# Norm factors moved into the exponentials, four weight blocks side by side at the start, and a fused last product

## The chip, the cores and the metric

The kernel runs on one core of a Trainium2 chip. The metric is the device time of one execution in microseconds (us). TensorE (PE) does the matmuls, VectorE (DVE) and ScalarE (ACT) the elementwise work, GpSimd (POOL) a little of it, and SyncE (SP) and ACT issue the transfers (DMA) between memory and the core. Each engine runs its own instructions in order and waits for others by semaphores.

## The reference

One decoder layer for 256 tokens of width 1024, all in float32:

```
hn = rmsnorm(h, mix_norm_g);  proj = hn @ w_in
a, b, q, k_c, v_c, k_s, v_s, k_w, v_w, gates = split(proj)
y_conv = silu(layernorm(depthwise_conv31(a * sigmoid(b))))
y_nsa  = gated sum of compressed, selected and window attention (8 heads of 64)
h = h + concat(y_conv, y_nsa) @ w_out
h = h + memory_attention(rmsnorm(h, mem_q_norm_g), rmsnorm(mem, mem_kv_norm_g))   # 4 heads of 256
h = h + peer(rmsnorm(h, peer_norm_g))   # 8 heads, top 16 of 128 x 128 keys, 16384 experts
out = rmsnorm(h, final_norm_g)
```

An RMS norm multiplies each token by its gain per channel and by one factor, rsqrt(mean(x*x) + eps). The factor of a token is the same for all channels, so it can be applied after the matmul, and for attention scores it can be applied to the score instead of to the query.

## The kernel before

Activations lie transposed: 128 channels on the partitions, 256 tokens along the row, eight such chunks (`KC` = 8) for a width of 1024. `hx` is x times the gain. A projection block gives 128 output channels and sums over the eight chunks. `proj1` does a block as eight float32 matmuls (16 passes of PE in the trace). `proj`, by `mm3` (L152 to L154), splits weight and activation into a high part (`hi`, made by ACT) and a rest (`lo`, made by DVE at L142) and does 24 matmuls. Weight blocks of 512 KB come in through `wload`, in four `raw` buffers; `hi` and `lo` have six buffers each.

The order on PE is the order in which the program is written. The order on DVE, ACT and SP is decided by a scheduler that knows estimated durations; each engine then keeps to it strictly.

At the start PE runs 14 warm-up matmuls, then blocks in pairs, `pb` and `pa` (the gate and the value of the convolution branch). For a norm, the class `Rstd` sums squares (`sa_`), `sums()` adds them over the partitions on PE (`ss_`), computes the factor on DVE in a chain of 13 small steps and makes two diagonal matrices (`dg_`). `rows()` spreads the factor over a row by matmuls with these (`sr_`), which ACT copies (`rs_`). The suffix is x for the input, m for the memory, h for the two later norms, c for the convolution's layer norm.

`conv_in` (L302 to L307) makes the convolution's input from `pb`, `pa` and the row of factors. The convolution itself is 124 instructions on DVE, called taps here (`yc`, L296 and L298), which the scheduler spreads over the next 100 us as filler between the splits `lo`, the scaling of memory keys (`mkt`, L440) and the maxima of the attention scores (`amx`, L559). When all taps are done, `lsum` (L607 to L610) adds the four channel groups and PE takes the mean over channels (`pmu`, L616).

Further on come the memory queries (`pmq`, eight chunks; `mq_out` scales and splits them), the expert layer's queries (`ppq`, sixteen chunks), the key scores and top-k, and then the experts' matmuls (`pu`, `pw`, `Y`), which fill the time from some 312 us to the end. At the end, each half of 128 tokens is normed from the two PSUM banks `Y` by L1049 to L1064 (`fz` the result, `fm` the factor, `fj` the squares).

Of the kernel before, what the change touches and what calls it, by code (L numbers as in the profile page):

```python
# [51 lines left out]
def constants():  # L52
# [44 lines left out]
def build(tc, A, out, dbg=None):
# [99 lines left out]
    class Rstd:  # L197
# [16 lines left out]
        def sums(self):  # L214
# [9 lines left out]
            rsqrt(y, m, t, sh)  # L224
            self.diag = mwk.tile([P, 2, P], F32, name=f"dg_{self.tag}", tag="rs_d", bufs=1)
# [85 lines left out]
    pend = []  # L311
    for i in range(4):
        pb = psum(T, f"pb{i}")
        wb = wload(A["w_in_t"][2 * i]) if i else w0
        proj1(pb, wb, hx)
        if i == 1:
            r0.sums()
        wa = wload(A["w_in_t"][2 * i + 1])
        if i == 0:
            nc.sync.dma_start(con1, A["con"][:, 0:NCON1])  # L320
        pa = psum(T, f"pa{i}")
        proj1(pa, wa, hx, range(4))
        if i == 1:
            r0.rows()
            conv_in(*pend)
# [845 lines left out]
```

## Time and profile before

| | |
|---|---|
| median of three runs | 1082.49 us (1081.4 to 1082.73) |
| the profiled execution | 1082.72 us |
| its span | 1080.9 us |
| PE, DVE, ACT, POOL busy | 1061.2, 871.8, 580.0, 102.3 us |

The span runs from the first to the last event of the trace, and 1.8 us of the time lie outside it. PE is busy in 98% of it. [...] DVE is busy in 81% over the whole: in eight or nine tenths of most slices up to some 700 us, and in six tenths after that. In the timeline, the number in brackets is how long the engine was idle before the instruction, and what ended that. The difference between two starts (the pitch) can be less than an instruction's length, since neighbours overlap.

### The profile page before, as it was taken

The numbers are of one execution on the slowest core, as the hardware profiler recorded it, in microseconds if no ns is written. First come the engines' busy times: TensorE is split into PE (matmuls) and PEld (weight loads), VectorE is DVE, ScalarE is ACT, GpSimd is POOL, SyncE is SP. The second block draws the span as 40 slices with busy tenths as digits, with TensorE's granted clock in tenths as the row PEclk, the third lists the DMA queues.
The fourth block names the chain that finished last, engine by engine and source line by source line (L and its number), as shares of the span: only waits on it lengthen the run. The fifth ranks groups of instructions, "written<-read, shape, count | busy, mean of one in ns | idle before, by whom it ended". The sixth has DMA issues, their size and how long they took to land.

```text
span 1080.9 us, 20534 instructions
## 1 busy us (share of the span) xinstructions
PE 1061.2 (98%) x7346; PEld 976.3 (90%) x7346; DVE 871.8 (81%) x2226; ACT 580.0 (54%) x1334; POOL 102.3 (9%) x82
## 2 busy tenths in 40 slices
PE   8999999999999999999999999999999999999997
PEld 7889878999999999999999999998888888888885
DVE  4998888978889998889999999986666666666665
ACT  4224676566455555665555555455555555555554
POOL 0000000000039992000000000001000000000000
PEclk9999999999999999999999999999999999999999
DMA  7744333525435555444554444466555555555552
GB/s 245 247 127 151 98 99 117 196 98 174 159 116 178 178 193 167 160 162 157 162 164 163 163 150 160 156 203 201 194 190 193 194 192 192 195 194 193 195 195 78
DMA packets 51685, 182.45 MB, mean 169 GB/s; under 512 B 5760, under 2 KB 6528, under 8 KB 51456
## 3 DMA queue, kind: packets, MB, share of 16 engines
q1 hardware_dynamic: 51296, 180.62, 50.8%
q8 instruction: 58, 0.95, 0.4%
q10 hardware_dynamic: 288, 0.52, 0.1%
q14 instruction: 43, 0.35, 0.1%
HBM read 179.81 MB, written 1.05 MB: 167 GB/s over the span
## 4 chain that ended last, share of the span: by engine, by line
PE 85%; DVE 13%; ACT 1%; DMA 1%; issue 0%; SPq 0%; DVEq 0%; ACTq 0%
PE Y L1071 32%; PE pu L152 9%; PE pu L154 8%; PE pu L153 8%; PE pq L163 2%; PE pw L1017 1%; PE ppq L152 1%; PE ppq L153 1%; PE ppq L154 1%; PE pb L163 1%; PE pw L1018 1%; PE pa L163 1%; DVE ohx L948 1%; PE pmk L152 1%; DVE lo L142 1%; DVE ohx L946 1%
## 5 line engine op out<-in xcount | busy, mean ns | idle before, releaser
L141 ACT ACTIVATE hi<-raw 128x512 fp32r<-128x512 f32 x624 | 376.7, 626 | 176.7 <-PE pu L153 66.9
L142 DVE TENSOR_TENSOR lo<-raw,hi 128x512 fp32r<-128x512 f32 x556 | 369.1, 687 | 26.8 <-ACT hi L141 21.0
L152 PE MATMUL pu<-hn_h,hi 128*128 128x256 f32 x1024 | 296.3, 289 | 0.0
L154 PE MATMUL pu<-hn_h,lo 128*128 128x256 f32 x1024 | 290.7, 284 | 1.9 <-DVE lo L142 1.9
L153 PE MATMUL pu<-hn_l,hi 128*128 128x256 f32 x1024 | 290.7, 284 | 0.0
L154 PEld LDWEIGHTS pu<-hn_h,lo 128*128 128x128 f32 x1024 | 197.3, 193 | 2.1 <-DVE lo L142 2.1
L153 PEld LDWEIGHTS pu<-hn_l,hi 128*128 128x128 f32 x1024 | 197.4, 193 | 0.0
L152 PEld LDWEIGHTS pu<-hn_h,hi 128*128 128x128 f32 x1024 | 197.2, 193 | 0.0
L1071 PE MATMUL Y<-hi,al 128*128 128x512 f32 x512 | 158.3, 389 | 0.0
L1071 PE MATMUL Y<-lo,ah 128*128 128x512 f32 x512 | 158.3, 389 | 0.0
L1071 PE MATMUL Y<-hi,ah 128*128 128x512 f32 x512 | 158.2, 389 | 0.0
L1071 PEld LDWEIGHTS Y<-hi,al 128*128 128x128 f32 x512 | 96.1, 188 | 20.0
L1071 PEld LDWEIGHTS Y<-lo,ah 128*128 128x128 f32 x512 | 96.1, 188 | 19.9
L1071 PEld LDWEIGHTS Y<-hi,ah 128*128 128x128 f32 x512 | 96.1, 188 | 19.8
L167 DVE TENSOR_TENSOR al<-slB,ah 128x256 fp32r<-128x256 f32 x88 | 37.4, 425 | 86.1 <-PE Y L1071 86.1
L166 ACT ACTIVATE ah<-slB 128x256 fp32r<-128x256 f32 x88 | 36.8, 418 | 110.7 <-PE Y L1071 110.7
L142 POOL TENSOR_TENSOR lo<-raw,hi 128x512 fp32r<-128x512 f32 x68 | 94.8, 1421 | 11.8 <-ACT hi L141 9.2
L1023 ACT ACTIVATE slB<-pw 128x348 f32<-128x348 f32 (+31 forms) x64 | 32.5, 507 | 70.2 <-DVE slB L1022 57.0
L298 DVE SCALAR_TENSOR_TENSOR yc<-u,par,yc 128x256 f32<-128x256 f32 x120 | 54.8, 474 | 0.1
L167 DVE TENSOR_TENSOR al<-slA,ah 128x256 fp32r<-128x256 f32 x40 | 17.1, 428 | 37.3 <-PE Y L1071 37.3
L166 ACT ACTIVATE ah<-slA 128x256 fp32r<-128x256 f32 x40 | 16.7, 418 | 49.3 <-PE Y L1071 48.0
L152 PE MATMUL ppq<-gx_h,hi 128*128 128x256 f32 x128 | 37.4, 292 | 0.0
(372 smaller groups left out, 1745.7 us busy)
## 6 DMA issues: line engine op xcount, KB each, us to landing
raw<-u SPq DMA_DIRECT2D x128, 512.0 KB, 3.4
raw<-v SPq DMA_DIRECT2D x128, 512.0 KB, 3.3
raw<-peer_w_q SPq DMA_DIRECT2D x16, 512.0 KB, 3.3
raw<-w_in_t SPq DMA_DIRECT2D x15, 512.0 KB, 3.8
raw<-w_mem_k SPq DMA_DIRECT2D x8, 512.0 KB, 4.5
raw<-w_mem_v SPq DMA_DIRECT2D x8, 512.0 KB, 3.3
raw<-w_out SPq DMA_DIRECT2D x8, 512.0 KB, 3.4
raw<-w_mem_q SPq DMA_DIRECT2D x8, 512.0 KB, 3.5
```

The lines of the kernel that those rows point to most:

```text
L141: S.activation(hi, r, AF.Copy)
L142: (engs or (V, V))[q].tensor_sub(lo, r, hi.bitcast(F32))
L152: PE.matmul(ps, w[0], xh, start=start, stop=False)
L153: PE.matmul(ps, w[0], xl, start=False, stop=False)
L154: PE.matmul(ps, w[1], xh, start=False, stop=stop)
L163: PE.matmul(ps, w[0][:, k * P:(k + 1) * P], x[:, k], start=k == 0, stop=k == KC - 1)
L166: S.activation(dst[0], src, AF.Copy)
L167: V.tensor_sub(dst[1], src, dst[0].bitcast(F32))
L298: V.scalar_tensor_tensor(yc[:, i], u[:, i, j:j + T], w, yc[:, i], op0=ALU.mult, op1=ALU.add)
L946: V.tensor_tensor(o4, o4, tif[:, side].unsqueeze(2).to_broadcast([P, 16, 16, 8]), op=ALU.mult)
L1023: S.activation(slB[:, done - J:, n0:n0 + 4].rearrange("p i n -> p n i"), pw[:, :, done:], AF.Copy, scale=1.0 / GSC)
L1071: PE.matmul(Y[nh][c], lhs[:, sl], wc[c][t], start=False, stop=i == KEYS - 1 and lhs is a[1], skip_group_check=True)
```

## The change

There are five parts. (1) At the start the first four blocks are computed side by side: in each of the eight chunks, one matmul for each of four accumulators (`acc`). Their weights come in 16 transfers of 128 KB on SP, into tiles `wf` that use buffers of `hi` and `lo`; x comes in four transfers that ACT issues. The sums of squares follow behind the four blocks and the row of factors behind the fifth. The rope constants (`posf`, `ang`, `kk`, `St`, `Ct`), which stood at the very start, come after the input blocks; the second part of the constants (`con2`, with the causal mask among others) is loaded behind the last four blocks. (2) The NSA queries `qraw` stay without the norm's factor; the factor goes into the scale of the exponentials (`r8`, `r8n`). (3) The memory queries likewise (`r16`); `rows()` is not called there, and `mq_out` splits straight from PSUM. (4) The expert queries likewise (`r2c`). (5) At the end the second bank of each half is finished by one instruction of DVE with two factors, and the first by ACT.

```
 def wload(src, n=1024):
...
-        if cnt[0] == 1:
-            nc.sync.dma_start(raw[:, 0:512], src[:, 0:512])
-            nc.sync.dma_start(raw[:, 512:], src[:, 512:])
...
-    nc.sync.dma_start(xT[:, 0:2], A["xT"][:, 0:2])
-    nc.sync.dma_start(par, A["par"])
-    w0 = wload(A["w_in_t"][0])
...
+    nc.scalar.dma_start(par[:, 0:32], A["par"][:, 0:32])
+    first = [[wts.tile([P, 512], F32, name=f"wf{c}{h}", tag=("hi", "lo")[c // 2], bufs=6) for h in range(2)] for c in range(4)]
+    for q in range(4):
+        nc.scalar.dma_start(xT[:, 2 * q:2 * q + 2], A["xT"][:, 2 * q:2 * q + 2])
+        for c in range(4):
+            o = 256 * (q % 2)
+            nc.sync.dma_start(first[c][q // 2][:, o:o + 256], A["w_in_t"][c][:, 256 * q:256 * q + 256])
...
+    acc = [psum(T, f"p{'ba'[c % 2]}{c // 2}", "mm" if c > 1 else "at") for c in range(4)]
+    for k in range(KC):
+        for c in range(4):
+            PE.matmul(acc[c], first[c][k // 4][:, (k % 4) * P:(k % 4 + 1) * P], hx[:, k], start=k == 0, stop=k == KC - 1)
+    r0.sums()
+    for i in range(2, 4):
+        pb = psum(T, f"pb{i}")
+        proj1(pb, wload(A["w_in_t"][2 * i]), hx)
+        if i == 2:
+            r0.rows()
+            conv_in(0, acc[0], acc[1])
+            conv_in(1, acc[2], acc[3])
+            conv(6)
+        pa = psum(T, f"pa{i}")
+        proj1(pa, wload(A["w_in_t"][2 * i + 1]), hx)
+        conv_in(i, pb, pa)
+        conv(6)
+    nc.sync.dma_start(con2, A["con"][:, NCON1:])
...
-        V.tensor_mul(dst, ps, r0.row)
+        if i < 2:
+            V.tensor_mul(dst, ps, r0.row)
+        else:
+            S.activation(dst, ps, AF.Copy)
...
-        V.tensor_scalar(mx, mx, -0.125, None, op0=ALU.mult)
+        V.tensor_scalar(mx, mx, r8n[:, hf:hf + 1], None, op0=ALU.mult)
...
-            S.activation(pe[:, b, 0:W], ps[:, b], AF.Exp, scale=0.125, bias=mx[:, b:b + 1], accum_out=sm[:, b:b + 1])
+            S.activation(pe[:, b, 0:W], ps[:, b], AF.Exp, scale=r8[:, hf:hf + 1], bias=mx[:, b:b + 1], accum_out=sm[:, b:b + 1])
...
 def mq_out(i, ps):
-        t = twk.tile([P, T], F32, name=f"mqt{i}", tag="mqt", bufs=4)
-        V.tensor_mul(t, ps, r1.row)
-        S.activation(mq_h[:, i], t, AF.Copy)
-        V.tensor_sub(mq_l[:, i], t, mq_h[:, i].bitcast(F32))
+        split((mq_h[:, i], mq_l[:, i]), ps)
...
+    for i in range(KC):
         mq_out(i, mq_chunk(i))
+        if i == 1:
+            r1.sums(rows=False)
...
-        V.tensor_mul(qt, ps, r2.row)
+        S.activation(qt, ps, AF.Copy)
...
-            V.tensor_mul(z[:, c * 512:c * 512 + 512], Y[nh][c], gfin[:, c * 512:c * 512 + 512])
+            if c == 0:
+                V.tensor_mul(z[:, 0:512], Y[nh][0], gfin[:, 0:512])
...
-        V.tensor_scalar(z[:, 0:512], z[:, 0:512], y, None, op0=ALU.mult)
-        nc.sync.dma_start(rows[:, 0:512], z[:, 0:512])
-        S.activation(z[:, 512:], z[:, 512:], AF.Copy, scale=y)
-        nc.scalar.dma_start(rows[:, 512:], z[:, 512:])
+        V.scalar_tensor_tensor(z[:, 512:], Y[nh][1], y, gfin[:, 512:], op0=ALU.mult, op1=ALU.mult)
+        nc.sync.dma_start(rows[:, 512:], z[:, 512:])
+        S.activation(z[:, 0:512], z[:, 0:512], AF.Copy, scale=y)
+        nc.scalar.dma_start(rows[:, 0:512], z[:, 0:512])
```

Three places show how the order on an engine moves. A row is a line of the program, an operation, what it writes and what it reads; a trailing xN stands for N like it. Line numbers differ between the two programs (the `lo` of L142 is at L134 after, the tap of L298 at L274).

PE at the start, before: whole blocks one behind the other.

```order
L163 MATMUL pb_169<-hx,raw_111 128x256 x8
L163 MATMUL pa_181<-hx,raw_178 128x256 x8
L163 MATMUL pb_190<-hx,raw_191 128x256 x8
L218 MATMUL ss_x<-ones,sa_x 128x1 x2
L163 MATMUL pa_226<-hx,raw_224 128x256 x4
L233 MATMUL sr_x<-dg_x,ones 128x128 x2
```

After: the last two rounds of one matmul for each of the four blocks, and what follows.

```order
L290 MATMUL pb_177<-hx,wf_115 128x256
L290 MATMUL pa_178<-hx,wf_117 128x256
L290 MATMUL pb_175<-hx,wf_111 128x256
L290 MATMUL pa_176<-hx,wf_113 128x256
L290 MATMUL pb_177<-hx,wf_115 128x256
L290 MATMUL pa_178<-hx,wf_117 128x256
L210 MATMUL ss_x<-ones,sa_x 128x1 x2
L155 MATMUL pb_234<-hx,raw_235 128x256 x8
L227 MATMUL sr_x<-dg_x,ones 128x128 x2
```

The sums of squares `ss_x` move from behind the third block to behind the fourth, and `sr_x`, the row of factors, from the middle of the fourth to behind the fifth.

DVE ahead of the convolution's mean, before: the last tap is two rows behind the last `amx` in this stretch.

```order
L565 RECIPROCAL asm300_1616<-asm300_1616 128x2
L142 TENSOR_TENSOR lo351_1807<-raw35_1800,hi351_1806 128x512
L298 SCALAR_TENSOR_TENSOR yc_168<-u_166,par_64,yc_168 128x256
L566 TENSOR_TENSOR asm300_1616<-asm300_1616,gate_652 128x2
L559 TENSOR_REDUCE amx301_1668<-pss301_1662 128x2
L298 SCALAR_TENSOR_TENSOR yc_168<-u_166,par_64,yc_168 128x256
L560 TENSOR_SCALAR amx301_1668<-amx301_1668 128x2
L142 TENSOR_TENSOR lo360_1867<-raw36_1864,hi360_1866 128x512
L609 TENSOR_TENSOR lsum2_1659<-yc_168 128x256
L142 TENSOR_TENSOR lo361_1871<-raw36_1864,hi361_1870 128x512
L610 TENSOR_TENSOR lsum_1657<-lsum_1657,lsum2_1659 128x256
L565 RECIPROCAL asm301_1672<-asm301_1672 128x2
```

After: this is the stretch that ends with the last `lsum`, and begins behind the same `amx` (the one of the sixth pair, 301).

```order
L562 TENSOR_SCALAR amx301_1689<-amx301_1689,r81_673 128x2
L274 SCALAR_TENSOR_TENSOR yc_174<-u_172,par_64,yc_174 128x256
L134 TENSOR_TENSOR lo301_1716<-raw30_1709,hi301_1715 128x512
L274 SCALAR_TENSOR_TENSOR yc_174<-u_172,par_64,yc_174 128x256
L567 RECIPROCAL asm301_1693<-asm301_1693 128x2
L134 TENSOR_TENSOR lo310_1824<-raw31_1821,hi310_1823 128x512
L274 SCALAR_TENSOR_TENSOR yc_174<-u_172,par_64,yc_174 128x256
L568 TENSOR_TENSOR asm301_1693<-asm301_1693,gate_669 128x2
L134 TENSOR_TENSOR lo311_1828<-raw31_1821,hi311_1827 128x512
L611 TENSOR_TENSOR lsum2_1680<-yc_174 128x256
L573 TENSOR_SCALAR ape301_1692<-ape301_1692,asm301_1693 128x256
L612 TENSOR_TENSOR lsum_1678<-lsum_1678,lsum2_1680 128x256
```

Behind that `amx` stand four taps (three of them in these rows) where one stood. Counted from the maximum before it (`amx300`) to the last `lsum`, there are 11 taps and 5 `lo` where there were 5 and 3. In the same way the number of taps ahead of the first `lo` of the memory keys falls from 80 to 68.

PE between the third and the fourth chunk of the memory queries, before, with the matmuls that spread the row of factors between them:

```order
L153 MATMUL pmq2_2398<-g1_l_1957,hi471_2405 128x256
L154 MATMUL pmq2_2398<-g1_h_1956,lo471_2406 128x256
L233 MATMUL sr_h1_2433<-dg_h1_2360,ones_65 128x128 x2
L152 MATMUL pmq3_2450<-g1_h_1956,hi480_2453 128x256
L153 MATMUL pmq3_2450<-g1_l_1957,hi480_2453 128x256
L154 MATMUL pmq3_2450<-g1_h_1956,lo480_2454 128x256
```

After, without them:

```order
L145 MATMUL pmq2_2424<-g1_l_1978,hi431_2431 128x256
L146 MATMUL pmq2_2424<-g1_h_1977,lo431_2432 128x256
L144 MATMUL pmq3_2461<-g1_h_1977,hi440_2464 128x256
L145 MATMUL pmq3_2461<-g1_l_1978,hi440_2464 128x256
L146 MATMUL pmq3_2461<-g1_h_1977,lo440_2465 128x256
```

## Rows read from the trace of the kernel before

**Rows 1.** The page of the profile: busy us, share and instructions of each engine

```profile
PE 1061.2 (98%) x7346; PEld 976.3 (90%) x7346; DVE 871.8 (81%) x2226; ACT 580.0 (54%) x1334; POOL 102.3 (9%) x82
```

**Rows 2.** All waits of PE: engine, line, releaser, total us, times, longest

```profile
PE sr_c L233 <- DVE dg_c L227: 2.3, 1, 2.3
PE pb L163 <- DVE hx L259: 2.1, 1, 2.1
PE pu L154 <- DVE lo L142: 1.9, 1, 1.9
PE sr_h L233 <- DVE dg_h L227: 1.4, 1, 1.4
PE pmu L616 <- DVE asm L565: 1.1, 1, 1.1
```

**Rows 3.** Timeline of PE, 0 to 36 us: start, length, instructions, idle before

```profile
6.90 1.03 PE L163 MATMUL pb<-hx,raw 128*128 128x256 f32 x4
10.00 4.53 PE L163 MATMUL pb<-hx,raw 128*128 128x256 f32 x12 [2.07 <-DVE hx L259]
...
21.27 0.50 PE L218 MATMUL ss_x<-ones,sa_x 128*128 128x1 f32 x4
...
24.51 0.71 PE L233 MATMUL sr_x<-dg_x,ones 128*128 128x128 f32 x4 [0.90 <-DVE dg_x L227]
...
26.79 3.62 PE L163 MATMUL pb<-hx,raw 128*128 128x256 f32 x16
30.24 3.62 PE L163 MATMUL pa<-hx,raw 128*128 128x256 f32 x16
```

**Rows 4.** Windows: busy time by engine, granted clock, DMA share, GB/s

```profile
10.00:12.00 2.00, 2.00 (x5) 1.64 (x6) 2.00 (x8) 1.36 (x4) 0.00 (x0) 0.50 1.03 412
26.00:35.00 9.00, 9.00 (x44) 7.93 (x43) 8.88 (x26) 5.09 (x13) 0.00 (x0) 1.00 0.96 340
65.00:75.00 10.00, 10.00 (x48) 8.57 (x47) 10.00 (x29) 0.83 (x2) 0.00 (x0) 1.00 0.38 102
168.00:172.00 4.00, 3.90 (x33) 3.93 (x34) 2.91 (x10) 2.48 (x8) 0.00 (x0) 1.00 0.03 11
420.00:422.00 2.00, 2.00 (x11) 2.00 (x11) 1.93 (x6) 0.63 (x1) 0.00 (x0) 0.50 0.74 252
```

**Rows 5.** Waits of DVE between 25.7 and 152.1 us, the largest

```profile
DVE mkt L440 <- PE pmk L154: 2.9, 5, 0.9
```

**Rows 6.** Timeline of DVE at the start

```profile
25.68 0.42 DVE L302 TENSOR_TENSOR tb<-pb,rs_x 128x256 f32<-128x256 f32 x1 [0.16 <-ACT rs_x L235]
```

**Rows 7.** Timeline of DVE before the convolution's sums, 146 to 152 us

```profile
146.13 0.42 DVE L559 TENSOR_REDUCE amx<-pss 128x2 f32<-128x256 f32 x1
...
147.01 0.48 DVE L298 SCALAR_TENSOR_TENSOR yc<-u,par,yc 128x256 f32<-128x256 f32 x1
147.41 0.61 DVE L571 TENSOR_SCALAR ape<-ape,asm 128x256 f32<-128x256 f32 x2
...
151.46 0.68 DVE L142 TENSOR_TENSOR lo<-raw,hi 128x512 fp32r<-128x512 f32 x1
152.06 0.42 DVE L610 TENSOR_TENSOR lsum<-lsum,lsum 128x256 f32<-128x256 f32 x1
```

**Rows 8.** Timeline of PE at the memory queries

```profile
205.87 0.28 PE L154 MATMUL pmq<-g_h,lo 128*128 128x256 f32 x1
...
207.97 0.36 PE L152 MATMUL pmq<-g_h,hi 128*128 128x256 f32 x1
```

**Rows 9.** Timeline of the end

```profile
1073.96 0.69 DVE L1050 TENSOR_TENSOR fz<-Y,gfin 128x512 f32<-128x512 f32 x1
...
1074.75 0.48 DVE L1061 TENSOR_SCALAR fz<-fz,fm 128x512 f32<-128x512 f32 x1
...
1076.86 0.72 ACT L1063 ACTIVATE fz<-fz,fm 128x512 f32<-128x512 f32 x1 [1.39 <-DVE fm L1059]
```

More of the change, by code (lines that the diff above doesn't have):

```diff
@@ L224, in sums @@
             rsqrt(y, m, t, sh)
+            if not rows:
+                return
             self.diag = mwk.tile([P, 2, P], F32, name=f"dg_{self.tag}", tag="rs_d", bufs=1)
@@ L309, in conv_in @@
             taps.append(lambda j=j: tap(i, j))
-    pend = []
-    for i in range(4):
-        pb = psum(T, f"pb{i}")
[L314 to L320, printed above, removed]
-        pa = psum(T, f"pa{i}")
[L322 to L325, printed above, removed]
-        proj1(pa, wa, hx, range(4, KC))
-        if i == 0:
-            pend = (i, pb, pa)
-        else:
-            conv_in(i, pb, pa)
+    acc = [psum(T, f"p{'ba'[c % 2]}{c // 2}", "mm" if c > 1 else "at") for c in range(4)]
@@ L331, in build @@
         conv(6)
     nc.sync.dma_start(con2, A["con"][:, NCON1:])
-    S.activation(St, ang, AF.Sin, scale=Pm("sgn"))
-    S.activation(Ct, aabs, AF.Sin, scale=-1.0, bias=halfpi)
+    posi = wk.tile([P, T], I32, name="posi", tag="rt")
+    nc.sync.dma_start(posi, A["pos"].partition_broadcast(P))
+    Ct = ch.tile([P, T], F32, name="Ct")
+    St = ch.tile([P, T], F32, name="St")
+    posf = wk.tile([P, T], F32, name="posf", tag="tb")
+    V.tensor_copy(posf, posi)
+    ang = wk.tile([P, T], F32, name="ang", tag="th")
@@ new lines, in build @@
+    V.tensor_scalar(ang, posf, C("inv"), None, op0=ALU.mult)
+    kk = wk.tile([P, T], F32, name="kk", tag="ta")
+    MAGIC = 12582912.0
+    V.tensor_scalar(kk, ang, 1.0 / (2.0 * math.pi), MAGIC, op0=ALU.mult, op1=ALU.add)
+    V.tensor_scalar(kk, kk, MAGIC, None, op0=ALU.subtract)
+    c1 = 6.28125
+    c2 = float((np.array([2.0 * math.pi - c1], np.float32).view(np.uint32) & np.uint32(0xFFFFF000)).view(np.float32)[0])
+    c3 = 2.0 * math.pi - c1 - c2
+    for c in (c1, c2, c3):
+        V.scalar_tensor_tensor(ang, kk, -c, ang, op0=ALU.mult, op1=ALU.add)
@@ L335, in build @@
+    PIF = 3.1415925
+    V.tensor_scalar(ang, ang, PIF, -PIF, op0=ALU.min, op1=ALU.max)
+    halfpi = cst.tile([P, 1], F32, name="halfpi")
+    V.memset(halfpi, math.pi / 2)
+    S.activation(St, ang, AF.Sin, scale=C("sgn"))
+    V.scalar_tensor_tensor(kk, ang, -1.0, ang, op0=ALU.mult, op1=ALU.max)
+    S.activation(Ct, kk, AF.Sin, scale=-1.0, bias=halfpi)
     S.activation(halfpi, Ct[:, 0:1], AF.Tanh)
@@ L419, in build @@
     V.tensor_scalar(chalf, r0.col, 0.5, None, op0=ALU.mult)
+    r8, r8n = [ch.tile([P, 2], F32, name=f"r8{j}") for j in range(2)]
+    V.tensor_scalar(r8, r0.col, 0.125, None, op0=ALU.mult)
+    V.tensor_scalar(r8n, r0.col, -0.125, None, op0=ALU.mult)
     for hf in range(2):
@@ L763, in m_weighted @@
             split((mo_h[:, i], mo_l[:, i]), po)
-    pq0 = mq_chunk(0)
-    r1.sums()
-    pq1 = mq_chunk(1)
-    pq2 = mq_chunk(2)
-    r1.rows()
-    mq_out(0, pq0)
-    mq_out(1, pq1)
-    mq_out(2, pq2)
-    for i in range(3, KC):
+    r16 = [mp.tile([P, 2], F32, name=f"r16{j}") for j in range(2)]
+    for i in range(KC):
         mq_out(i, mq_chunk(i))
+        if i == 1:
+            r1.sums(rows=False)
+            for j in range(2):
+                V.tensor_scalar(r16[j], r1.col, (0.0625, -0.0625)[j], None, op0=ALU.mult)
         if i == 4:
@@ L821, in build @@
     show("h2", h2T)
+    r2c = tk.tile([P, 2], F32, name="r2c")
     skp = tp.tile([P, 16, P], F32, name="skp")
```

66 lines of the change are left out of this document (19 added, 47 removed).

## The prediction

> **What bounds the kernel now.** I read the page first. TensorE (PE) is busy 1061 of 1080.9 us, DVE 872, ACT 580 [rows 1]. Time can come from PE's work, its waits, its slow stretches, and the few microseconds before its first and after its last matmul. The change takes next to no work from PE, so I read its waits next: some 12 us in all, the five longest in [rows 2]. Three stand where the change works: the first block's wait for `hx` (2.1), that of `sr_h` for the diagonals (1.4), that of `pmu` for DVE (1.1).
>
> Then the start, instruction by instruction [rows 3]. A block of the input projection is 16 passes, and the next starts 3.45 us behind it (26.79, 30.24): 0.216 a pass. From 6.90 to 33.69 (30.24 + 3.45) PE does six blocks, 20.7 us, and two small steps, 0.37 (`ss_x`) and 0.55 (`sr_x`): 21.6 us of work in 26.8. The 5.2 us between are a gap behind the first four passes (10.00 less 7.76: 2.2), twelve passes that take 4.4 instead of 2.6 because the granted clock is 0.50 from 10 to 12 us [rows 4] (1.8), and the gap ahead of `sr_x` (1.1, of which the view names 0.90 a wait for `dg_x`).
>
> Last, DVE beside it. From 26 us on it is full: 8.88 of 9, then 10.00 of 10 in the window from 65 to 75 [rows 4]. Between `tb` (25.68 [rows 6]) and the last `lsum` (152.06 [rows 7]) lie 126.4 us, of which it waits only 9.5, in nine groups, all behind PE or ACT; the largest is 2.9 us in five pieces [rows 5], and before 78 us there is next to none. Its filler is the 124 taps, and `pmu` needs every one of them.
>
> **Start.** Side by side, the 64 passes of four blocks take 13.8 us. Per quarter of the contraction they need 0.75 MB (0.5 of weights, 0.25 of x). At 412 or 340 GB/s [rows 4] that is 1.8 to 2.2 us, beside 3.45 us of PE. If the loads and `hx` keep up, the first two losses go: 2.2 + 1.8 = 4.0 us. If they are late, none of it comes; I take 4.0, as the loads have a margin of a third. The diagonals `dg_x` now have one block (3.45) to hide under. In the trace 3.2 us pass from `ss_x` (21.27) to `sr_x` [rows 3], but DVE's order now has four pieces of the memory's norm (`mg_l`, `sa_m`, some 0.4 each, part of it in the gaps of the small chain) ahead of them. So PE will still wait, 0.4 where it lost 1.1. Start: 4.7 us (bounds 0 and 5.2).
>
> [...]
>
> **What the start meets at `pmu`.** PE, 4.7 us earlier, needs DVE 4.7 us earlier too, and up to some 141 us DVE's order provides for that: ahead of the first `lo` stand 12 taps fewer. But they aren't gone. The rope constants (nine instructions, before at 9 to 15 us in idle time) now stand in the full stretch, and the taps that made room stand behind the last waits for PE. From the `amx` that was at 146.13 to the last `lsum` DVE had 5 taps and 3 `lo`; now it has 11 and 5, and the first `lsum` and one more `ape`. The prices are pitches from [rows 7]: a tap 0.40 (147.01 to 147.41), a `lo` 0.60 (151.46 to 152.06), `lsum` 0.34 and half an `ape` pair 0.26. That is 6 x 0.40 + 2 x 0.60 + 0.34 + 0.26 = 4.2, with a small one 4.3. Up to that `amx` DVE follows PE (its waits stay), behind it PE follows DVE. So `pmu` comes 4.7 - 4.3 = 0.4 us earlier, and the rest of the start is a new wait of PE: some 2 us at a `pmv` for a late `lo`, and 3 to 4 at `pmu`, in place of 1.1. The least is nothing (all given back), the most is 4.7 (second rival).
>
> PE's clock: waits of 2.1 and 1.9 were followed by a clock of 0.50 (10 to 12 and 420 to 422 us [rows 4]), the wait of 2.3 at `sr_c` [rows 2] was not (1.00 from 168 to 172 us [rows 4]). So the new wait may cost 1.8 us, as it did at the start, or nothing; with matmuls between its two pieces I give that one chance in three and take nothing. [...]
>
> **Memory queries.** `sr_h`, both `dg_h`, the row's copy and eight products `mqt` go. PE's last `pmq` before is at 205.87, the next is at 207.97 [rows 8], 0.12 is the usual distance: 2.0 us. Nothing of the norm remains that PE waits for: `r16` is used three chunks later. Against it, `mq_l` now stands ahead of a `lo` that was just in time, 0.3 to 0.4. Bounds 1.6 and 2.0; I take 2.0, since the eight products leave the same queue.
>
> **Other norm factors.** Four DVE products of `qraw` and 16 of `pqt`, some 0.41 each, become ACT copies of about the same length. PE waits for none of these (no such line among its waits), and ACT is busy 54% [rows 1]: 0. The exponentials get a scale from a tile in place of a constant. They do read a bias tile already; 0 to 0.1 us each beside other work: 0. The wait of `pu` for `lo` (1.9) stands behind a long DVE chain in which nothing changes: 0, it only moves.
>
> **The end.** DVE's second `fz` product of each half goes (0.60 pitch at 1073.96), and so does `fz` at 1074.75 [rows 9], which stood in the last chain of small steps (some 0.3 of its 0.48, the rest fell in gaps). In their place the first half's fused product stands ahead of the last chain (0.6), while its own chain starts 0.58 earlier. Counted through, the last chain starts 0.3 earlier and is 0.3 shorter. The fused product itself isn't in the trace: from PSUM, 128x512, it is nearest to the product of 0.69, beside ACT's 0.72 in the same place. End: 0.6 us (0.2 to 1.0).
>
> **Sum** on the profiled execution, 1082.72 (span 1080.9 and 1.8 around it): 0.4 + 2.0 + 0.6 = 3.0, so 1079.7. The median is 0.2 lower, so I forecast 1079.5.
>
> **Rivals.**
> First, the forecast with the clock's drop behind `pmu`: 1.8 more, 1081.3. For it: two of three waits of this size. Against it: the two pieces. Chance 0.20, beside 0.36 for the forecast without it (own range 1078.5 to 1081.3).
> Second, DVE catches up and the start is kept whole. DVE waits 9.5 us before `pmu`; if taps run in that time, the last `lsum` is 4.7 us earlier as well: 4.7 + 2.0 + 0.6 = 7.3, so 1075.2. Against it: DVE executes in order, and the taps stand behind those waits, not in them. 0.22.
> Third, the other side: the start gains too little for what it costs at `pmu`. DVE's 4.3 us more behind that `amx` are paid in any case; with 2.6 from the other two places, the kernel is slower once the start gains less than 1.7. The place is DVE's queue: `causb` reads the second part of the constants, and it and `mg_l`, which reads the memory, now stand ahead of `dg_x`. These loads are queued behind some 5.8 MB. At 340 GB/s, with 3 us for the first, the constants land at 20 us, and DVE needs them at 21; below 320 GB/s each lost microsecond goes into `sr_x` and `tb`. At 250 they land at 26, the start gains nothing: 1082.5 + 1.7 = 1084.2, and with the clock's drop, likely behind a stall of 5 us at `sr_x`, 1086.0. Chance 0.12. [...]
> Fourth, the two small edits don't pay: the 2.0 at the queries reappears as a wait a chunk later, since DVE has `lo` after `lo` there. 1081.5 to 1082.3. 0.10.
>
> **Numbers.** A measurement of this kernel tells about 0.2% (2.2 us) from no change. Faster by that (under 1080.3): forecast and second rival, 0.58. Within it: first and fourth, 0.30. Slower (over 1084.7): third, 0.12. The range runs from the second rival's 1075.2, less 0.8 for a start of 5.2 and a better end, to 1083.4, between the fourth and the third: it leaves out the third and a still larger gain, under 0.2 together.
>
> **What would show it.** Right: 64 passes without a gap from 6.9 at a clock of 1.00, `tb` near 26 us, the seventh block starting at about 29.0 instead of 33.7; then a PE wait of 5 to 6 us in two pieces before and at `pmu`, with DVE full behind the `amx`, and the last `lsum` within 1 us of 152. At the queries, `pmq` at a distance of 0.12 across the place of `sr_h`. At the end, the last DMA about 5 us behind PE's last `Y`, as it is 0.6 shorter. Wrong: `lsum` near 147 (DVE's waits absorbed the taps), or `dg_x` behind `mg_l` waiting for a DMA.

## The result, and the profile after

| | before | after |
|---|---|---|
| median, us | 1081.95 (1080.44 to 1082.73) | 1097.44 (1094.04 to 1098.14) |
| span of the profiled execution | 1080.9 | 1095.5 |

The changed kernel is slower: the ratio of the times is 1.0139, with a 95% interval of 1.0114 to 1.0163. That is 15.5 us more, where 3.0 less was forecast.

The page of after has this row of busy times, to be read against [rows 1]. DVE has 7.8 us less work, ACT 7.1 more, and PE is busy 11.0 us longer with four instructions fewer:

```profile
PE 1072.2 (98%) x7342; PEld 977.0 (89%) x7342; DVE 864.0 (79%) x2199; ACT 587.1 (54%) x1353; POOL 101.6 (9%) x82
```

Next, the waits of PE in after (as in [rows 2]: releaser, total, times, longest):

```profile
PE pmu L618 <- DVE lsum L612: 3.1, 1, 3.1
PE sr_x L227 <- DVE dg_x L221: 3.1, 1, 3.1
PE pu L146 <- DVE lo L134: 2.6, 1, 2.6
PE sr_c L227 <- DVE dg_c L221: 2.4, 1, 2.4
PE pmv L456 <- DVE lo L134: 2.0, 1, 2.0
```

The waits for `hx` and at `sr_h` are gone, as the change says. There is a wait of 3.1 at `sr_x`, where it was 0.9, one of 2.0 at `pmv` is new, and that at `pmu` is 3.1, where it was 1.1. But these five make 13.2 us and the five of [rows 2] made 8.8, so waits explain less than a third of the loss. The timeline of PE in after shows where the rest is:

```profile
7.08 0.60 PE L290 MATMUL pb<-hx,wf 128*128 128x256 f32 x2
...
20.90 0.50 PE L210 MATMUL ss_x<-ones,sa_x 128*128 128x1 f32 x4
21.26 3.70 PE L155 MATMUL pb<-hx,raw 128*128 128x256 f32 x16
28.02 1.20 PE L227 MATMUL sr_x<-dg_x,ones 128*128 128x128 f32 x4 [3.06 <-DVE dg_x L221]
29.02 4.54 PE L155 MATMUL pa<-hx,raw 128*128 128x256 f32 x16
...
148.84 0.39 PE L456 MATMUL pmv<-lo,mg 128*128 128x256 f32 x1 [2.03 <-DVE lo L134]
...
157.50 1.19 PE L618 MATMUL pmu<-lsum,ones 128*128 128x256 f32 x2 [3.06 <-DVE lsum L612]
...
729.19 0.63 PE L1065 MATMUL Y<-hi,ah 128*128 128x512 f32 x2
...
1087.35 0.40 PE L1065 MATMUL Y<-hi,al 128*128 128x512 f32 x1
```

and the same two ends of the `Y` matmuls in the timeline of PE before:

```profile
724.84 0.63 PE L1071 MATMUL Y<-hi,ah 128*128 128x512 f32 x2
...
1072.80 0.39 PE L1071 MATMUL Y<-hi,al 128*128 128x512 f32 x1
```

Before, the 1536 `Y` matmuls take 1072.80 + 0.39 - 724.84 = 348.4 us, 0.2268 each; after, 358.6, 0.2334 each. No wait stands between them in either, and the granted clock, which the profile gives as a share of full speed, is 1.00 over the whole stretch of both (windows from 726 to 1070 and from 731 to 1085 us). The same instructions, as many of them, simply run 3% slower: 10.2 us. That is 70% of the 14.6 us that the span grew by, and the change edits nothing there.

Taking the starts of some matmuls from both timelines and subtracting gives where the 14.6 us of span came from:

| stretch | forecast, us | measured, us |
|---|---|---|
| up to the first `pkv` (40.60 to 40.30) | -4.7 | -0.3 |
| from there to `pmu` (152.62 to 157.50) | +4.3 | +5.2 |
| `pmu` to the sums of the layer norm `ss_c` | 0 | +2.8 |
| `ss_c` to the first `pmq` | 0 | -0.4 |
| first `pmq` to the first score `pms` (213.80 to 219.00) | -2.0 | -2.1 |
| `pms` to the first `Y` | 0 | -0.85 |
| the `Y` matmuls | 0 | +10.2 |
| end of `Y` to the span's end | -0.6 | 0.0 |

**The start.** The timeline of DVE in after shows why PE waits at `sr_x`, and further on the stretch ahead of `pmu`:

```profile
24.27 0.23 DVE L544 CAST causb<-con 128x128 bf16<-128x128 f32 x1 [7.77 <-DMA con<-con]
24.41 0.15 DVE L212 TENSOR_SCALAR m_x<-ss_x 128x2 f32<-128x2 f32 x1
...
26.09 0.48 DVE L233 SCALAR_TENSOR_TENSOR mg_l<-mT,par,mg 128x256 fp32r<-128x256 f32 x1
...
27.60 0.48 DVE L221 TENSOR_SCALAR dg_x<-con,rsc_x 128x128 f32<-128x128 f32 x2
...
29.68 0.42 DVE L278 TENSOR_TENSOR tb<-pb,rs_x 128x256 f32<-128x256 f32 x1
...
145.41 0.40 DVE L561 TENSOR_REDUCE amx<-pss 128x2 f32<-128x256 f32 x1
...
154.60 0.17 DVE L567 RECIPROCAL asm<-asm 128x2 f32<-128x2 f32 x1 [1.10 <-ACT ape L566]
...
156.94 0.42 DVE L612 TENSOR_TENSOR lsum<-lsum,lsum 128x256 f32<-128x256 f32 x1
```

PE has the sums `ss_x` done at 21.4, but DVE stands 7.8 us at `causb`, the cast of the causal mask, until the second part of the constants lands at 24.2. Only then does the chain of the norm begin, 3 us late, and with it `tb`, with which the convolution's work on DVE begins: at 29.68, where it was at 25.68 [rows 6]. From there to the last `lsum` DVE needs 127.3 us now (to 156.94) and needed 126.4 before (to 152.06 [rows 7]). So `pmu` is 4.9 later mainly because DVE begins 4.0 later. Windows of after (busy time by engine, granted clock, DMA share, GB/s) show the loads and the clock:

```profile
4.00:24.00 20.00, 20.00 (x97) 18.04 (x97) 5.85 (x18) 4.39 (x9) 0.26 (x1) 1.00 0.95 314
28.00:30.00 2.00, 1.98 (x7) 1.82 (x8) 1.86 (x6) 1.61 (x6) 0.00 (x0) 0.50 0.96 352
150.00:155.00 5.00, 4.44 (x23) 3.83 (x22) 3.90 (x10) 2.46 (x9) 0.00 (x0) 0.66 0.44 138
155.00:160.00 5.00, 2.50 (x8) 1.65 (x9) 5.00 (x14) 0.94 (x4) 0.00 (x0) 0.72 0.55 177
160.00:165.00 5.00, 5.00 (x24) 4.51 (x24) 2.70 (x9) 3.72 (x12) 0.00 (x0) 0.60 0.28 97
```

The loads ran at 314 GB/s from 4 to 24 us, just under the 320 below which the third rival sets in. Behind the wait at `sr_x` the clock is 0.50 (28 to 30 us), and behind those at `pmv` and `pmu` it is 0.66, 0.72 and 0.60 in the three windows from 150 to 165. Before it was 1.00 in all three of these.

### The profile page after: what moved, and what is told of

The parts are those of the page before. It is cut to its first block, busy times and chain, and to the rows that moved or that the text cites. A ratio compares the mean times of both kernels' runs of the same rounds, so it can differ in the third digit from the quotient of the medians.

```text
span 1095.5 us, 20541 instructions
## 1 busy us (share of the span) xinstructions
PE 1072.2 (98%) x7342; PEld 977.0 (89%) x7342; DVE 864.0 (79%) x2199; ACT 587.1 (54%) x1353; POOL 101.6 (9%) x82
## 4 chain that ended last, share of the span: by engine, by line
PE 85%; DVE 12%; DMA 2%; ACT 1%; issue 0%; SPq 0%; ACTq 0%; DVEq 0%
PE Y L1065 32%; PE pu L144 9%; PE pu L146 8%; PE pu L145 8%; PE pq L155 2%; PE pw L1010 1%; PE ppq L145 1%; PE ppq L144 1%; PE ppq L146 1%; PE pw L1011 1%; DVE ohx L941 1%; DMA mT<-memT 1%; PE pmk L144 1%; DMA xT<-xT 1%; PE pa L155 1%; PE pmw L145 1%
## 5 line engine op out<-in xcount | busy, mean ns | idle before, releaser
L134 DVE TENSOR_TENSOR lo<-raw,hi 128x512 fp32r<-128x512 f32 x556 | 369.2, 688 | 32.1 <-ACT hi L133 28.3
L1065 PE MATMUL Y<-hi,ah 128*128 128x512 f32 x512 | 161.8, 396 | 0.0
L1065 PE MATMUL Y<-hi,al 128*128 128x512 f32 x512 | 161.8, 396 | 0.0
L1065 PE MATMUL Y<-lo,ah 128*128 128x512 f32 x512 | 161.8, 396 | 0.0
L134 POOL TENSOR_TENSOR lo<-raw,hi 128x512 fp32r<-128x512 f32 x68 | 93.8, 1403 | 11.8 <-ACT hi L133 9.1
L274 DVE SCALAR_TENSOR_TENSOR yc<-u,par,yc 128x256 f32<-128x256 f32 x120 | 55.8, 475 | 0.0
```

The source lines that it names most:

```text
L134: (engs or (V, V))[q].tensor_sub(lo, r, hi.bitcast(F32))
L274: V.scalar_tensor_tensor(yc[:, i], u[:, i, j:j + T], w, yc[:, i], op0=ALU.mult, op1=ALU.add)
L1065: PE.matmul(Y[nh][c], lhs[:, sl], wc[c][t], start=False, stop=i == KEYS - 1 and lhs is a[1], skip_group_check=True)
```

## The experiments

### Why the `Y` matmuls are slower

What the change can still alter in these matmuls is where their operands lie. In the built programs, per partition and in bytes (the traces show no addresses):

```
            before                      after
hi          36128                       19744    (first taken as wf)
lo          48416                       32032
raw         19744                       44320
ah, al      130848 ...                  130880 ...
```

Two things differ. The four blocks use buffers of `hi` and `lo` first, which puts these in front of `raw`. And `r2c`, the 8 bytes of factors of the expert layer, takes a place of 32 bytes in its pool (`tk`) and moves all behind it by as much, `ah` and `al` among them: the weights of the `Y` matmuls, whose moving operand is `hi` or `lo`. Theory: the 32 bytes; rivals: the order of `raw`, `hi` and `lo`, or something of the time (clock, loads). Four kernels undo or do one of the two.

**after_raw_first**: after, with the buffers of `raw` in front again.

```
+    wts.tile([P, 1024], F32, name="raw00", tag="raw", bufs=4)
     first = [[wts.tile([P, 512], F32, name=f"wf{c}{h}", ...
```

> The changed kernel with the weight buffers placed in the core's memory as in the kernel before (raw, hi, lo, instead of hi, lo, raw); nothing else differs. The Y matmuls start 0.2268 us apart before and 0.2333 after the change, 1559 of them: 10.1 us. If the place of hi and lo sets that pace, Y goes back to 0.227 and the time falls by about 10 us to some 1087. If the shift of the expert slices by 32 bytes sets it, or something else does, Y stays at 0.233 and the time at 1097.

**after_no_shift**: after, with `r2c` in another pool (`tp`), where it moves neither `ah` nor `al`.

```
-    r2c = tk.tile([P, 2], F32, name="r2c")
+    r2c = tp.tile([P, 2], F32, name="r2c")
```

> The changed kernel with the small factor tile r2c in another pool, so that everything behind it (the slices ah and al among it) lies at the addresses of the kernel before; hi, lo and raw stay as changed. If the shift by 32 bytes slows the Y matmuls, they go back from 0.233 to 0.227 us and the time falls by 10 us to some 1087. If the place of hi and lo does it, nothing moves: 1097.

**before_hi_first**: before, with `hi` and `lo` in front of `raw`.

```
+    wts.tile([P, 512], F32R, name="hi00", tag="hi", bufs=6)
+    wts.tile([P, 512], F32R, name="lo00", tag="lo", bufs=6)
     w0 = wload(A["w_in_t"][0])
```

> The kernel before with its weight buffers placed as in the changed one (hi, lo, raw); nothing else differs. If their place sets the pace of Y, Y slows from 0.227 to 0.233 us and the time rises by 10 us to some 1092. Otherwise 1082 and 0.227.

**before_shift**: before, with nothing but the tile `r2c`, which is set to zero and not used.

```
+    r2c = tk.tile([P, 2], F32, name="r2c")
+    V.memset(r2c, 0.0)
     skp = tp.tile([P, 16, P], F32, name="skp")
```

> The kernel before with an additional tile of 8 bytes a row (written once, read by nobody) at the place where the changed one has r2c, so that all behind it lies 32 bytes higher. If that shift slows Y: 0.233 us and 1092. If not: 0.227 and 1082.

Measured (each ratio is to runs of before on the same chip, here and below): after_raw_first 1095.86 us, ratio 1.0124 (1.0094 to 1.0155); after_no_shift 1087.07, 1.0046 (1.0029 to 1.0063); before_hi_first 1082.85, 1.0007 (0.9996 to 1.0018); before_shift 1092.7, 1.0092 (1.0067 to 1.0117). An unused tile of 8 bytes costs the kernel of before 10 us, and moving it out of the way gives the changed kernel 10 back. The order of the buffers does nothing. The group of the `Y` matmuls in the pages (busy, mean ns of one, idle ahead) shows it, first in before, then in after, in before_shift and in after_no_shift:

```profile
L1071 PE MATMUL Y<-hi,ah 128*128 128x512 f32 x512 | 158.2, 389 | 0.0
```

```profile
L1065 PE MATMUL Y<-hi,ah 128*128 128x512 f32 x512 | 161.8, 396 | 0.0
```

```profile
L1073 PE MATMUL Y<-hi,ah 128*128 128x512 f32 x512 | 161.8, 396 | 0.0
```

```profile
L1065 PE MATMUL Y<-hi,ah 128*128 128x512 f32 x512 | 158.0, 389 | 0.0
```

One matmul is 389 or 396 ns long, and follows its neighbour by 0.227 or 0.233 us.

What about the 32 bytes matters: the address of `ah` and `al` itself, or its distance to `hi` and `lo`? In before, that distance is 130848 - 36128 = 94720 = 185 x 512. The tiles that the program places from `hi` to `ah` add up to the same: 24576 bytes of `hi` and `lo`, 16384 of activations, 2048 in `tk`, 40960 of `slA` and 10752 in `tmp`. Six more kernels of before change one or the other.

**before_shift64** and **before_shift128**: `r2c` of 64 and of 128 bytes (`[P, 16]` and `[P, 32]` in the edit above).

> The kernel before with an additional tile of 64 bytes a row, so that all behind it lies 64 bytes higher: the slices ah and al keep their place within 64 bytes (32), which the tile of 8 bytes had moved to 0. If the place within 64 bytes decides the pace of Y: 0.227 us and 1082. If any shift does it: 0.233 and 1092.

> The kernel before with an additional tile of 128 bytes a row at the place of r2c: all behind it lies 128 bytes higher, so ah and al keep their place within 128 bytes (32), which shifts by 32 and 64 had changed. If the place within 128 bytes decides: 0.227 us and 1082. If any other address than that of before is slow: 0.233 and 1092.

**before_ah_only**: 32 bytes directly ahead of `ah`, so that only `ah`, `al` and what stands behind them move. **before_ah_512**: the same with 512 bytes (`[P, 128]`).

```
+        if i == 0:
+            pad = tmp.tile([P, 8], F32, name="pad", tag="pad", bufs=1)
+            G.memset(pad, 0.0)
         ah = tmp.tile([P, T], F32R, name=f"ah{i}", tag="ah")
```

> The kernel before with a tile of 32 bytes a row directly ahead of the four buffers ah and al, the operands that PE loads as weights for Y: these (and the small tiles of the end behind them) lie 32 bytes higher, all else where it was. If the addresses of ah and al set the pace of Y: 0.233 us and 1092. If another of the tiles that both earlier shifts moved does it (o, ua, slA, h2T): 0.227 and 1082.

> The kernel before with 512 bytes more directly ahead of ah and al: the shifts by 32, 64 and 128 were slow. If the address within 512 bytes counts: 0.227 us and 1082. If not: 0.233 and 1092.

**before_all32**: 32 bytes ahead of everything, `hi` and `lo` too, so that all distances stay.

```
+    pad = cst.tile([P, 8], F32, name="pad")
+    V.memset(pad, 0.0)
     cnt = [0]
```

> The kernel before with 32 bytes more ahead of the weight buffers, so that raw, hi, lo, the slices, ah and al all lie 32 bytes higher and keep their distances to each other. If the distance between the weights ah, al and the moving operands hi, lo sets the pace of Y: 0.227 us and 1082. If the address of ah and al itself does: 0.233 and 1092.

**before_ah_low**: `ah` and `al` first in their pool, 10752 = 21 x 512 bytes lower.

```
     tmp = outer.enter_context(tc.tile_pool(name="tmp", ...))
+    for t in ("ah", "al"):
+        tmp.tile([P, T], F32R, name=f"{t}x", tag=t)
```

> The kernel before with ah and al placed ahead of the other tiles of their pool, 10752 bytes (21 x 512) lower; these lie 4 KB higher in turn. If only the low part of the address counts (within 512 bytes it is the same): 0.227 us and 1082. If any address but that of before is slow: 0.233 and 1092.

The third column is the time from the first `Y` to the end of the last, divided by 1536. The granted clock was 1.00 from 800 to 900 us, within this stretch, in each of these twelve kernels.

| kernel | distance of `ah` to `hi`, rest by 512 | us from one `Y` to the next | ratio to before |
|---|---|---|---|
| before | 0 | 0.2268 | |
| before_hi_first | 0 | 0.2268 | 1.0007 (0.9996 to 1.0018) |
| after_no_shift | 0 | 0.2268 | 1.0046 (1.0029 to 1.0063) |
| before_all32 (`ah` itself 32 off) | 0 | 0.2268 | 0.9991 (0.9973 to 1.0009) |
| before_ah_low | 0 | 0.2268 | 1.0001 (0.9988 to 1.0014) |
| before_ah_512 | 0 | 0.2268 | 1.0003 (0.9988 to 1.0017) |
| after, after_raw_first | 32 | 0.2334, 0.2334 | 1.0139, 1.0124 (intervals above) |
| before_shift, before_ah_only | 32 | 0.2334, 0.2334 | 1.0092 (above), 1.0084 (1.0065 to 1.0103) |
| before_shift64 | 64 | 0.2334 | 1.0077 (1.0058 to 1.0096) |
| before_shift128 | 128 | 0.2325 | 1.0081 (1.0057 to 1.0104) |

The pair that decides is before_ah_only and before_all32. In the first only the weights move, in the second weights and moving operand together, both by 32 bytes:

```profile
L1071 PE MATMUL Y<-hi,ah 128*128 128x512 f32 x512 | 161.8, 396 | 0.0
```

```profile
L1074 PE MATMUL Y<-hi,ah 128*128 128x512 f32 x512 | 158.0, 389 | 0.0
```

So it is the distance between the two operands, not the address of one. For `Y`, a distance that is a multiple of 512 bytes was fast in six kernels (0.2268 us), one that is 32, 64 or 128 off was slow in six (0.2325 to 0.2334). A distance 256 off wasn't tried. Why the distance counts is open: no run shows the cause.

The 32 bytes don't slow every matmul. By the order of the pools in the program `r2c` also moves `mg` and `mg_l`, operands of the memory keys' matmuls `pmk`, against `hi` and `lo`. These are 256 columns wide, and got shorter, 279 ns where they took 283; first before, then before_shift:

```profile
L153 PE MATMUL pmk<-mg_l,hi 128*128 128x256 f32 x64 | 18.1, 283 | 0.0
```

```profile
L153 PE MATMUL pmk<-mg_l,hi 128*128 128x256 f32 x64 | 17.9, 279 | 0.0
```

In before_ah_only and before_all32, where the distance of these two isn't changed, they take 282.

### What the other parts are worth

**before_mq_end**: before, with two parts of the change alone, the memory queries (third) and the end (fifth).

```
+        split((mq_h[:, i], mq_l[:, i]), ps)
...
+            V.tensor_scalar(mx, mx, r16[1][:, hf:hf + 1], None, op0=ALU.mult)
...
+        V.scalar_tensor_tensor(z[:, 512:], Y[nh][1], y, gfin[:, 512:], op0=ALU.mult, op1=ALU.mult)
+        nc.sync.dma_start(rows[:, 512:], z[:, 512:])
```

> The kernel before with two parts of the change alone: the memory queries' factor in the exponentials, and the fused product at the end. The slices stay at the addresses of before. If both are worth what I forecast, 2.0 and 0.6 us: 1082.2 - 2.6 = 1079.6, with no wait of 1.4 us at sr_h. If the wait of the queries only moves to a later chunk and the two last transfers get into each other's way: 1081.5 to 1082.5.

Measured: 1079.57 us over 11 runs, ratio 0.9965 (0.9954 to 0.9976). It beats both kernels. Its waits of PE have no `sr_h`, and those of the start and of `pmu` stand as in [rows 2]:

```profile
PE pu L154 <- DVE lo L142: 2.6, 1, 2.6
PE sr_c L235 <- DVE dg_c L229: 2.3, 1, 2.3
PE pb L163 <- DVE hx L261: 2.0, 1, 2.0
PE pmu L618 <- DVE asm L567: 1.1, 1, 1.1
```

`pmu` starts 0.1 later than before and `pms` 2.06 earlier: the two microseconds of the queries, to the tenth. Another 0.8 is gained from the first `pu` to the first `pw`, in this kernel as in after. It is the clock: behind the wait of `pu` for `lo`, 1.9 long, it was 0.50 before [rows 4], and behind the one of 2.6 here it stayed at 1.00:

```profile
419.00:421.00 2.00, 2.00 (x19) 2.00 (x18) 1.93 (x6) 1.19 (x3) 0.00 (x0) 1.00 0.75 262
```

In after_no_shift a wait of the same 2.6 was followed by 0.50 (424 to 426 us), so these 0.8 aren't shown to come from the edits. From PE's end to the span's end it takes 7.5 us where before took 7.7. That would be 0.2 for the end, not 0.6; but the six other executions with the new end took 7.75 to 7.9, and nine with the old one 7.7 to 7.8, so no gain of the end is shown.

**fewer_taps**: after_no_shift with 12 of the 124 taps left out, so that part of the convolution isn't computed; it asks whether DVE's work ahead of `pmu` is what PE waits for there.

```
-        for j in range(TAPS):
+        for j in range(TAPS - 3):
             taps.append(lambda j=j: tap(i, j))
```

> The changed kernel without the shift by 32 bytes, and with 12 of the convolution's 124 taps left out (the last three of each channel group): 4.7 us of DVE's work less. No tap stands behind amx300 any more. If DVE's late taps make PE wait at pmu, that wait (2.6 us) and the one at pmv (2.0) go, with the slow clock behind them, and the time falls from 1087.1 by 6 to 8 us to some 1080. If PE waits there for something else, it stays within 1 us of 1087.

Measured: 1077.8 us, ratio 0.994 (0.992 to 0.9961). In this run the start is worth little, with the longest wait at `sr_x` of all, and still `pmu` comes 1.9 earlier than before and without a wait; `pms` comes 5.1 earlier:

```profile
27.46 0.68 PE L227 MATMUL sr_x<-dg_x,ones 128*128 128x128 f32 x4 [3.45 <-DVE dg_x L221]
...
150.70 0.60 PE L618 MATMUL pmu<-lsum,ones 128*128 128x256 f32 x2
```

On DVE, `tb` is as late as in the changed kernel, but the stretch to the last `lsum` is 119.0 us long, where after_no_shift took 127.3:

```profile
28.89 0.41 DVE L278 TENSOR_TENSOR tb<-pb,rs_x 128x256 f32<-128x256 f32 x1
...
147.92 0.42 DVE L612 TENSOR_TENSOR lsum<-lsum,lsum 128x256 f32<-128x256 f32 x1
```

By the ratios this kernel is 1.1% faster than after_no_shift, 11 us, where 6 to 8 were expected; the two traces differ by 7.6.

**loads_early**: after_no_shift, with the second constants issued by ACT behind x, and the memory's loads behind that of the fifth block.

```
+    nc.scalar.dma_start(con2, A["con"][:, NCON1:])
     nc.sync.dma_start(con1, A["con"][:, 0:NCON1])
```

> The changed kernel without the shift by 32 bytes, and with the second part of the constants and the memory loaded earlier (the constants by ACT behind x, the memory behind the fifth block's weights). The planner's order of the taps moves with it: 77 stand ahead of the first lo (68 in the changed kernel, 80 before), and 6 behind the maximum amx300 (11 and 5). If late loads cost the start its gain and the order of the taps took the rest, dg_x no longer waits for a load, the seventh block starts at about 29.5 us instead of 30.6, pmu comes about 4 us earlier than before the change, and the time is some 1076 to 1077. If DVE's total work sets pmu, whatever the order, PE waits there for 4 us and the time is 1082 to 1084.

Measured: 1082.6 us, ratio 0.9989 (0.9978 to 1.0). The start did not get better: `sr_x` waits 3.01, now because all of the memory's norm (`mg_l`, `sa_m`, as many pairs as chunks) stands on DVE ahead of `m_x`, which begins at 25.05. One late thing was exchanged for another, and the first `pkv` is 1.1 later than before. The time lies where it was expected if DVE's total work sets `pmu`. The gain over after_no_shift lies at `pmu`, where the wait is 1.9, without a drop of the clock behind it (1.00 in the windows from 152 to 162 us). From `tb` (29.48) to the last `lsum` DVE needs 124.4 us here, since the memory's norm is done before `tb`.

**start_clear** takes both out of the way: constants and positions on ACT behind x, the rope constants back ahead of the four blocks, and the memory's norm held behind `conv_in(1)`.

```
+    nc.scalar.dma_start(con2, A["con"][:, NCON1:])
+    nc.scalar.dma_start(posi, A["pos"].partition_broadcast(P))
...
             conv_in(1, acc[2], acc[3])
+            for k in range(KC):
+                tc.keep_in_program_order(gain_split(mg[:, k], mg_l[:, k], mT[:, k], ...))
+                rm.add(mT[:, k])
             conv(6)
```

> The changed kernel without the shift by 32 bytes, with the second part of the constants and the positions loaded by ACT behind x, the rope constants back in DVE's idle time ahead of the sums, the memory loaded behind the fifth block's weights, and its norm held behind conv_in on DVE, so that nothing but the chain of the factor stands between ss_x and dg_x. If the start's loss is what stands ahead of dg_x: the wait at sr_x is under 0.6 us, the clock stays at 1.00 and pv comes 4 to 4.7 us earlier than before. Of the taps 114 stand ahead of amx300 (113 in the changed kernel, 119 before), so by the theory of the taps 2 to 3 us of that are given back at pmu: pmu 1.5 to 2.5 us earlier than before, 2.0 more at the queries, 0.6 at the end: 1077 to 1078. If pmu keeps what the start gives: 1075. If the start stays slow for another reason: 1081 or more.

Measured: 1082.21 us over 12 runs, ratio 0.9989 (0.9978 to 0.9999). Here the start works. The timeline of PE:

```profile
20.56 0.50 PE L212 MATMUL ss_x<-ones,sa_x 128*128 128x1 f32 x4
20.92 3.70 PE L155 MATMUL pb<-hx,raw 128*128 128x256 f32 x16
24.46 0.61 PE L229 MATMUL sr_x<-dg_x,ones 128*128 128x128 f32 x4
25.17 3.72 PE L155 MATMUL pa<-hx,raw 128*128 128x256 f32 x16
...
151.28 1.19 PE L618 MATMUL pmu<-lsum,ones 128*128 128x256 f32 x2 [2.86 <-DVE lsum L612]
```

No wait at `sr_x`, and the first `pkv` starts at 35.64, 4.96 earlier than before. But `pmu` is only 1.34 earlier, so 3.6 went back there. DVE shows why:

```profile
25.52 0.42 DVE L283 TENSOR_TENSOR tb<-pb,rs_x 128x256 f32<-128x256 f32 x1 [1.36 <-ACT rs_x L231]
...
150.71 0.43 DVE L612 TENSOR_TENSOR lsum<-lsum,lsum 128x256 f32<-128x256 f32 x1
```

The row of factors stands one and a half blocks further back in PE's order, so `tb` is only 0.2 earlier than before although PE is 5 us ahead, and from there DVE needs 125.2 us. The windows show the clock behind the wait at `pmu`:

```profile
150.00:155.00 5.00, 3.72 (x14) 2.87 (x15) 4.09 (x12) 0.75 (x2) 0.00 (x0) 0.50 0.44 168
155.00:160.00 5.00, 5.00 (x33) 4.05 (x32) 3.18 (x8) 3.66 (x11) 0.00 (x0) 0.85 0.24 79
```

By these windows an estimated 3.72 x 0.50 + 5.00 x 0.15 = 2.6 us of PE's work is lost, and `ss_c` is 0.95 later than before. From there to the first `pmq` another 1.1 is lost, with a clock of 0.76 behind the wait at `sr_c` (168 to 172 us). With the queries' 2.1 us, `pms` stands where it did (-0.04). The start was cleared and the time is still not the 1077 to 1078 that was expected: as DVE's work is placed here, the start's 5 us on PE are worth nothing.

## Why the prediction was wrong

**Other norm factors: 0.** This is the step that failed most. Its instructions cost what I took: the copies on ACT took 0.383 (`qraw`) and 0.365 us (`pqt`) where the products on DVE had taken 0.416, an exponential of the NSA scores (`ape`) 0.513 instead of 0.430 (medians), and the stretch from `pms` to the first `Y`, where the expert queries lie, is no longer than before. But `r2c` is a tile, I priced the instructions of the edit and not its bytes, and those cost 10.2 us in matmuls that never touch it. No rival had a place for it: I had said that time can come from PE's work, its waits, its slow stretches and the two ends, and never asked whether the same matmuls would run at the same rate. Here `Y` takes 0.227 or 0.233 us by nothing but the distance between the weights and the moving operand.

**Start: 4.7 forecast, 0.3 measured.** The first half of the step holds: 64 passes run from 7.08 to 20.90, 0.216 each, at a clock of 1.00 (the window from 4 to 24 us), and the two losses of 2.2 and 1.8 are gone. In the trace the 16 pieces of 128 KB landed 4.2 us after their issue (median, 2.5 to 4.9) and kept up with PE. The second half failed: I let PE wait 0.4 at `sr_x`; it waited 3.1, and the clock behind it cost 1.4 more (1.00 for `sr_x` and 4.37 for the next block, where 0.52 and 3.45 are usual). With `sr_x` came `tb`, at 29.68 where I had it near 26. The place is the one the third rival names: `causb`, put ahead of the norm on DVE, waiting for constants that land at 24.2 where 21 was needed. I gave it 0.12 since 340 GB/s would just do; it was 314. The rival's price was 1084.2 to 1086.0 us; the kernel without the 32-byte shift, 1087.07, is just beyond it. So apart from the addresses, the third rival comes nearest. Its condition, a start that gains less than 1.7, held in after, but not in the profiled execution of after_no_shift: there the first `pkv` is 3.05 earlier than before, and `pmu` is 3.3 later all the same, with `tb` 2.4 later. In four executions with this same start (after, after_raw_first, after_no_shift, fewer_taps) `sr_x` waits 3.06, 1.92, 1.57 and 3.45, and `causb` has its constants at 24.3, 22.9, 22.8 and 23.6, so how much is lost varies from run to run.

**What the start meets at `pmu`: 4.3 forecast, 5.2 measured.** That PE waits for DVE there holds: with 12 taps fewer the wait is gone (fewer_taps). From that `amx` to the last `lsum` it was 5.93 us [rows 7] and is 156.94 - 145.41 = 11.53, so 5.6 more, where I had 4.3. In it DVE waits 1.1 for an exponential of ACT; ACT itself had stood 2.5 us, until 152.84, for PE to be done with a `pmv`. But I counted only what stands behind that `amx`, and the taps there are taps that DVE no longer does ahead of it. Over the whole stretch from `tb` to the last `lsum` the order is worth little: 126.4 us before, 127.3 in after and after_no_shift, 125.2 in start_clear, all with 124 taps. What places `pmu` is where `tb` begins. I had PE 4.7 us earlier and `tb` where it was; in after PE is 0.3 earlier and `tb` 4.0 later. From the first `pkv` to `pmu` it takes 3.6 more than before in start_clear and 6.3 in after_no_shift, so that 5.2 lies near 4.3 is in part luck. The two pieces of the new wait, 2.0 and 3.1, were forecast as some 2 and 3 to 4. The second rival, that DVE catches up, is refuted by start_clear.

**The clock behind it: nothing taken, 2.8 measured** (from `pmu` to `ss_c`, where PE waits for nothing). The first rival was right on this, and low: 1.8 was one stretch of 2 us, but here the clock was 0.66, 0.72 and 0.60 in three windows of 5 us. It also dropped behind `sr_x`, to 0.50.

**Queries: 2.0 forecast, 2.1 measured** in after, and 2.06 alone in before_mq_end. The wait didn't reappear; the fourth rival falls there.

**End: 0.6 forecast, nothing shown.** The chain was shortened as counted: from PE's end to the last issue 4.42 before, 3.78 after. But from that issue to the span's end it takes 3.97 instead of 3.29. After's last steps, all engines:

```profile
1090.78 0.75 DVE L1055 SCALAR_TENSOR_TENSOR fz<-Y,fm,gfin 128x512 f32<-128x512 f32 x1
1090.78 0.72 ACT L1057 ACTIVATE fz<-fz,fm 128x512 f32<-128x512 f32 x1 [1.69 <-DVE fm L1053]
...
1091.53 0.38 ACTq L1058 DMA_DIRECT2D out<-fz  x1
```

The fused product takes 0.75 (0.69 was my nearest row) and ends when ACT's does, so that both last transfers are issued together (1091.53 and 1091.56), where one had been ahead (1077.37 and 1077.61). That this is why they land later is argued, not shown.

## What to carry to other kernels

When a change adds, removes or moves a tile, compare the mean length of the largest matmul groups before looking at any wait: an unused 8 bytes cost 1% here, and a changed distance between weights and moving operand showed as the same instructions running slower with nothing ahead of them. A gain ahead of the full engine wasn't kept here: DVE needed 124 to 127 us from `tb` to the last `lsum` in the kernels with all taps, so the start's 5 us were lost at `pmu` as long as `tb` began where it had, with the clock's drop on top. With less for DVE to do in it, 119 us in fewer_taps, `pmu` came 1.9 earlier than before. Of five parts made at once, two measured apart gave 0.35%, of which the trace puts 2 us down to the queries and 0.8 to a clock that happened to stay up; that is the version to keep.

## What the runs showed of the hardware

- The `Y` matmuls (float32, 128x128 by 512 columns) repeated every 0.227 us where weights and moving operand lay a multiple of 512 bytes apart in a partition (six kernels), and every 0.232 to 0.233 us where they lay 32, 64 or 128 bytes off that (six kernels). Other matmuls didn't follow this: the 256-wide `pmk` (the group with `mg_l` and `hi`) were shorter with `r2c`'s 32 bytes (279 ns in before_shift and after, 283 in before), and the 256-wide `pu`, whose operands `r2c` doesn't move, were alike (288 ns in after, 289 before, in the group with `hn_h` and `hi`).
- PE's clock fell behind idle stretches of 3.45 us (`sr_x` in fewer_taps, 0.50 from 30 to 32), 3.06 (`sr_x` in after, 0.50 from 28 to 30), 2.86 (`pmu` in start_clear, 0.50 from 150 to 155), 2.32 (`sr_c` in start_clear, 0.76 from 168 to 172) and 1.92 (`sr_x` in after_raw_first, 0.50 from 28 to 30). It stayed at 1.00 behind 1.57 (`sr_x` in after_no_shift, 26 to 36), 1.87 (`pmu` in loads_early, 152 to 162) and the 2.3 at `sr_c` in before (168 to 172 [rows 2, 4]). Behind the wait of `pu` for `lo` it stayed at 1.00 after 2.57 in after (424 to 432) and 2.6 in before_mq_end (419 to 421), and fell to 0.50 after 1.91 in before (420 to 422) and 2.6 in after_no_shift (424 to 426). The same waits at `sr_c` and `pu` went both ways, so length alone didn't decide.
- In after a load landed late with much queued ahead of it: SP needed 10.3 us to issue the 16 loads of the four blocks, issued the second constants (417 KB) at 14.1, and they landed 10.1 us later. Some 5.9 MB had been issued by then, these included; at the 314 GB/s of the window from 4 to 24 us, that much is in at an estimated 23 us, so by this estimate what was queued ahead accounts for nearly all of the delay.
